# A top-10 index kernel: the last three tiles laid over 16 partitions a row, with a new order of the tail

## The chip, the cores and the metric

The kernel runs on one core of a Trainium2 chip. The metric is the device time of one execution in microseconds (us), and lower is better. The profiled span of a kernel is about 1.8 us shorter than its device time: the kernel before has 684.3 us in the profile and 686.1 us on the clock of that run. Times inside a profile count from the start of its span.

## The reference

For each of 8192 rows of 8192 random fp32 numbers: the indices of the ten largest, largest first.

```python
def reference(x, k):                       # x: (8192, 8192) fp32, k = 10
    indices = np.argpartition(x, -k, axis=1)[:, -k:]
    values = np.take_along_axis(x, indices, axis=1)
    sorted_idx = np.argsort(-values, axis=1)
    return np.take_along_axis(indices, sorted_idx, axis=1)   # int64
```

## The kernel before

The 64 tiles have 128 rows each (4.19 MB). A row lies over R = 8 partitions, W = 1024 numbers in each, so one SBUF tile holds S = 8 groups of A = 16 rows. A tile passes through these stages:

1. **Weigh.** ScalarE (ACT) takes exp(36 (x - 4.7)), and TensorE (PE) adds up those weights over the eight partitions of a row: 1024 chunk sums a row. A chunk with a large number in it has a large sum.
2. **Choose.** VectorE (DVE) takes the 12 best chunks of a row, in five passes over the sums.
3. **Gather, mask, extract.** GpSimd (POOL) fetches the eight numbers of each chosen chunk, DVE and POOL mask them to the row they belong to, and 12 small PE matmuls (24 rows of the profile; together the *extract* of a tile) bring them together: 12 x 8 = 96 candidates a row.
4. **Rank.** DVE takes the ten best candidates.
5. **Finish.** For a batch of eight tiles DVE turns positions into indices in seven steps; PE matmuls (the *deliveries*, two rows of the profile for each tile of the batch) bring them into rows of the output; a cast and a store follow.

The parts that the change and the argument touch, with cuts marked:

```python
epool = ...tile_pool(name="e", bufs=3)       # weights between ACT and PE: three buffers
xpool = ...tile_pool(name="x", bufs=4)       # x tiles
spsum = ... bufs=2    # chunk sums in PSUM
gpsum = ... bufs=3    # candidates in PSUM
fpsum = ... bufs=1    # the accumulator of the deliveries
starts = list(range(0, ntiles, TB)) + [last - 2]   # batches of 8; the last are 56-60 and 61-63

def load(t):
    src = x[t * P:(t + 1) * P, :].rearrange("(s a) (q j) -> (a q) s j", a=A, q=R)  # runs of 4 KB
    ...
def weigh(t):
    parts = [S // 4, S // 4, S // 4, S // 8, S // 8] if t == last else [S // 2, S // 2]
    for h, n in enumerate(parts):            # an ACT pass, then its matmuls
        e = epool.tile([P, S // 2, W], bf16, tag="e", name="e")
        nc.scalar.activation(out=e..., in_=xts[t]..., func=ACTF.Exp, ...)
        # n x 2 matmuls of 128x512 into the sums
...
    for t in range(last):                    # the order in which every engine gets its work
        interleave(choose_steps(t), rank_steps(t - LAG) if LAG <= t < last - 1 else [])
        if t >= 1:
            spread(t - 1, 0 if t == last - 1 else G // 2)      # the mask, DVE and POOL
        gather(t)
        weigh(t + 1)
        if 1 <= t < last - 2:
            extract(t - 1)
        todo = {last - 4: 5, last - 3: TB + 2}.get(t, 3)
        run(later[:todo])                    # finish steps and deliveries of a batch
        ...
    extract(last - 3)                        # tile 60
    extract(last - 2)                        # tile 61
    run(choose_steps(last)); spread(last - 1); gather(last)
    extract(last - 1)                        # tile 62
    # ranks of 59, 60, 61; seven finish steps of 56-60; mask, extract and rank of 63
    run(steps[-2:])                          # cast and store of 56-60
    run(finish_steps(batch_of[last]))        # 61-63
```

## Time and profile before

| | us |
|---|---|
| time, median of four runs | 686.68 (685.10 to 687.15) |
| profiled span | 684.3 |
| load of x at 420 GB/s, up to about | 645 |
| tail after it, about | 39 |
| in the tail: sums of tile 63 ready | 653.47 |
| indices of 63 given to POOL | 660.62 |
| extract of 63 done | 672.78 |
| last delivery done | 680.38 |

Up to about 645 us the load sets the pace: it runs at 420 GB/s while no engine is full (from 40 to 600 us PE and DVE are busy for 84% of the time, ACT for 75%). What a change of compute and its order can shorten is the tail. It is read as a chain of times at which the last tile (63) passes each stage.

### The profile page before, as it was taken

The page shows a single profiled execution, that of the slowest core. Times are in us where ns is not written, and L with a number is a line of the kernel's source. Part 1 is how long each engine was busy: PE and PEld are TensorE (multiplying, and loading weights), DVE is VectorE, ACT ScalarE, POOL GpSimd, SP SyncE. Part 2 cuts the span into 40 slices and gives each one's busy share as a digit, 9 for nine tenths or more (in the row PEclk, how much of TensorE's full clock was granted, in tenths as well). Part 3 has the DMA queues.
Part 4 walks back from the last instruction along what each step waited for, and adds up shares of the span by engine and source line. Part 5 has one row for each costly group of instructions (what it writes and reads, how often), then busy time and mean ns, then how long its engine had stood idle before and what let it go on. Part 6 is the DMA issues. An engine that isn't in the chain of part 4 may idle for free.

```text
span 684.3 us, 7927 instructions
## 1 busy us (share of the span) xinstructions
PE 555.2 (81%) x2646; PEld 342.9 (50%) x2690; DVE 559.3 (82%) x1313; ACT 488.8 (71%) x264; POOL 183.4 (27%) x135
## 2 busy tenths in 40 slices
PE   2688878888877788887988798889788788788976
PEld 0245544555554455554654456556445445445564
DVE  1567868799878977789896998789987898789996
ACT  5777777777777767777777777787777777777810
POOL 0113223313331331322331333132233133223250
PEclk9765866669888888596786667777988858866775
DMA  8999999999999999999999999999999999999700
GB/s 354 421 420 419 420 421 419 421 419 421 418 421 419 420 420 419 420 420 420 420 420 419 421 419 420 420 419 421 420 420 419 420 419 414 420 420 420 287 1 6
DMA packets 70592, 269.69 MB, mean 394 GB/s; under 512 B 4374, under 2 KB 5014, under 8 KB 70550
## 3 DMA queue, kind: packets, MB, share of 16 engines
q1 hardware_dynamic: 69926, 268.62, 95.9%
q10 hardware_dynamic: 624, 0.56, 0.3%
q8 instruction: 21, 0.34, 0.2%
q14 instruction: 21, 0.17, 0.1%
HBM read 268.51 MB, written 0.66 MB: 393 GB/s over the span
## 4 chain that ended last, share of the span: by engine, by line
DMA 58%; PE 14%; DVE 11%; SPq 5%; ACT 5%; issue 4%; POOL 2%; ACTq 0%; DVEq 0%
DMA xt<-in_x_dram 56%; PE s L152 8%; SPq L94 5%; ACT e L144 5%; PE g L214 4%; DVE wall L171 2%; DMA out_dram<-opack 2%; POOL cand L185 2%; DVE m L172 2%; DVE cidb L176 1%; DVE cidb L174 1%; PE fo L254 1%; DVE wall L175 1%; DVE masked L203 1%; DVE rows L274 0%
## 5 line engine op out<-in xcount | busy, mean ns | idle before, releaser
L144 ACT ACTIVATE e<-xt,bias 128x4096 bf16<-128x4096 f32 (+2 forms) x131 | 475.5, 3630 | 155.9 <-DMA xt<-in_x_dram 147.6
L152 PE MATMUL s<-e,group 128*128 128x512 bf16 x980 | 342.7, 506 | 117.4 <-ACT e L144 112.7
L152 PEld LDWEIGHTS <-group 128*128 128x128 bf16 x1024 | 123.8, 124 | 311.3 <-issue 259.5
L214 PEld LDWEIGHTS g<-cpack,masked 128*128 128x128 f32 x1536 | 207.7, 215 | 20.1 <-issue 9.0
L214 PE MATMUL g<-cpack,masked 128*128 128x8 f32 x1536 | 199.7, 269 | 4.9 <-DVE posb L228 3.1
L185 POOL INDIRECT_COPY cand<-xt,idx 128x192 f32 x64 | 64.8, 1013 | 478.9 <-DMA xt<-in_x_dram 123.6
L171 DVE MAX8 wall<-s 128x8 f32<-128x1024 f32 x64 | 78.8, 1232 | 114.0 <-PE s L152 102.7
L203 POOL TENSOR_TENSOR masked<-cand,cpack 128x768 f32<-128x768 f32 x64 | 117.6, 1838 | 5.3
L174 DVE FIND_INDEX8 cidb<-wall,s 128x8 uint16<-128x1024 f32 x64 | 78.4, 1224 | 0.0
L176 DVE FIND_INDEX8 cidb<-wall,m 128x8 uint16<-128x1024 f32 x64 | 78.1, 1220 | 0.0
L172 DVE MATCH_REPLACE8 m<-wall,s 128x1024 f32<-128x1024 f32 x64 | 77.8, 1215 | 0.0
L175 DVE MAX8 wall<-m 128x8 f32<-128x1024 f32 x64 | 77.4, 1209 | 0.0
L203 DVE TENSOR_TENSOR masked<-cand,cpack 128x768 f32<-128x768 f32 (+1 forms) x63 | 60.2, 956 | 0.2 <-POOL cand L185 0.2
L254 PE MATMUL fo<-rows,send 128*64 128x160 f32 (+2 forms) x128 | 28.4, 372 | 3.0 <-DVE rows L274 3.0
L144 ACT ACTIVATION_READ_ACCUMULATOR e<-xt,bias 128x1 f32 x131 | 24.4, 186 | 0.0
L254 PEld LDWEIGHTS fo<-rows,send 128*64 128x64 f32 (+2 forms) x128 | 18.4, 158 | 5.6 <-issue 3.5
L228 DVE FIND_INDEX8 posb<-t8a,g 128x8 uint16<-128x96 f32 x64 | 16.5, 258 | 0.0
L230 DVE FIND_INDEX8 posb<-t8b,g 128x8 uint16<-128x96 f32 x64 | 16.2, 254 | 0.0
L225 DVE MAX8 t8a<-g 128x8 f32<-128x96 f32 x64 | 15.9, 249 | 0.0
L226 DVE MATCH_REPLACE8 g<-t8a,g 128x96 f32<-128x96 f32 x64 | 15.9, 248 | 0.0
L336 ACT ACTIVATE e<-tall,bias 128x64 f32<-128x64 f32 x1 | 0.3, 347 | 21.5 <-DVE tall L231 21.5
L229 DVE MAX8 t8b<-g 128x8 f32<-128x96 f32 x64 | 15.6, 244 | 0.0
(37 smaller groups left out, 105.0 us busy)
## 6 DMA issues: line engine op xcount, KB each, us to landing
xt<-in_x_dram SPq DMA_DIRECT2D x248, 1024.0 KB, 16.3
xt<-in_x_dram SPq DMA_DIRECT2D x16, 512.0 KB, 9.2
out_dram<-opack ACTq DMA_DIRECT2D x6, 80.0 KB, 5.3
out_dram<-opack SPq DMA_DIRECT2D x1, 80.0 KB, 4.6
cpack<-topk_cpack ACTq DMA_DIRECT2D x1, 68.5 KB
out_dram<-opack SPq DMA_DIRECT2D x1, 50.0 KB
out_dram<-opack SPq DMA_DIRECT2D x1, 30.0 KB
```

Of the source, the lines that this page charges most:

```text
L94: nc.sync.dma_start(out=dst[:, s:s + n, :], in_=src[:, s:s + n, :])
L144: nc.scalar.activation(out=e[:, 0:n, :].rearrange("p s j -> p (s j)"), in_=xts[t][:, s0 * W:(s0 + n) * W], func=ACTF.Exp, bias=bias[:, 0:1 ...
L152: nc.tensor.matmul(ss[t][:, j:j + BANK], lhsT=group[:, s0 + i, :], rhs=e[:, i, j:j + BANK], start=s0 + i == 0, stop=s0 + i == S - 1)
L171: lambda: nc.vector.max(out=w16[:, 0:8], in_=m),
L172: lambda: nc.vector.match_replace(out=m2, in_to_replace=w16[:, 0:8], in_values=m, imm_value=-1.0),
L174: lambda: nc.vector.max_index(out=cid[:, 0:8], in_max=w16[:, 0:8], in_values=m),
L175: lambda: nc.vector.max(out=w16[:, 8:16], in_=m2),
L176: lambda: nc.vector.max_index(out=cid[:, 8:16], in_max=w16[:, 8:16], in_values=m2),
L185: nc.gpsimd.add_instruction(mybir.InstIndirectCopy(name=nc.get_next_instruction_name(), ins=[nc.gpsimd.lower_ap(xts[t]), nc.gpsimd.lower_a ...
L203: eng.tensor_tensor(out=masked[t][:, g0:g1], in0=cand[:, g0:g1].unsqueeze(2).to_broadcast(shape), in1=own.rearrange("p (c s) -> p c s", s= ...
L214: nc.tensor.matmul(gs[t][:, c, :], lhsT=mk[:, c, :, :].rearrange("p a s -> p (a s)"), rhs=place, start=True, stop=True)
L254: nc.tensor.matmul(fo, lhsT=send[:, i, 0:n * S], rhs=rows[:, i].rearrange("p a k -> p (a k)"), start=i == 0, stop=i == n - 1)
```

## The change

The intent, as far as the diff tells it: in the last three tiles, where nothing hides DVE's work, halve the number of chunk sums (a row over 16 partitions, 512 chunks of 16 numbers), so that choosing takes half as long. The price is 2 KB runs in the load and 192 candidates to rank. The last batch gets an accumulator of its own, in a buffer of the chunk sums, so that it need not wait for the cast of the batch before. The order of the tail changes too: extract 60 and the deliveries of batch 48-55 move ahead of the sums of tile 63. Smaller parts are the masks of the last tiles, shared out anew between DVE and POOL, and one buffer in place of two for the finish steps. The core of the diff, with cuts marked:

```diff
+class Layout:
+    def __init__(self, r):
+        self.R, self.A, self.S, self.W = r, P // r, r, N // r
...
+    wide, thin = Layout(8), Layout(16)
+    def layout(t):
+        return thin if t >= ntiles - TAIL else wide        # TAIL = 3
...
+        if b == len(starts) - 1:
+            fo = spsum.tile([P, wide.W], fp32, tag="s", name="fo")
+        else:
+            fo = fpsum.tile([P, wide.A * KMAX], fp32, tag="fo", name="fo")
...
-            interleave(choose_steps(t), rank_steps(t - LAG) if LAG <= t < last - 1 else [])
+            interleave(choose_steps(t), rank_steps(t - LAG) if t >= LAG else [])
             if t >= 1:
-                spread(t - 1, 0 if t == last - 1 else G // 2)
+                spread(t - 1)
             gather(t)
             weigh(t + 1)
-            if 1 <= t < last - 2:
+            if 1 <= t < last - 1:
                 extract(t - 1)
-            todo = {last - 4: 5, last - 3: TB + 2}.get(t, 3)
+            todo = {last - 4: 5, last - 3: 2}.get(t, 3)
+            if t == last - 2:
+                todo = TB
             run(later[:todo])
...
-        extract(last - 3)
-        extract(last - 2)
+        run(rank_steps(last - 3))
         run(choose_steps(last))
         spread(last - 1)
         gather(last)
+        extract(last - 2)
         extract(last - 1)
...
-        spread(last, 8)
+        run(steps[:5])
+        run(rank_steps(last - 2))
+        spread(last, G)
+        run(steps[5:7])
         extract(last)
...
+        final = finish_steps(batch_of[last])
+        run(final[:-2])
         run(steps[-2:])
+        run(final[-2:])
```

More of the change, by code (lines that the diff above doesn't have):

```diff
@@ L12 @@
 N = 8192
-R = 8
-A = P // R
-S = P // A
-W = N // R
 BANK = 512
@@ L26 @@
 LAG = 3
-PAD = 96
+TAIL = 3
+PAD = 208
+class Layout:
+    def __init__(self, r):
+        self.R, self.A, self.S, self.W = r, P // r, r, N // r
 @with_exitstack
@@ L57 @@
     out_u32 = out.bitcast(u32)
-    out_rows = out_u32.rearrange("(r a) n -> r (a n)", a=A)
+    wide, thin = Layout(8), Layout(16)
     consts = ctx.enter_context(tc.tile_pool(name="consts", bufs=1))
@@ L62 @@
     small = ctx.enter_context(tc.tile_pool(name="small", bufs=2))
-    bpool = ctx.enter_context(tc.tile_pool(name="batch", bufs=2))
+    bpool = ctx.enter_context(tc.tile_pool(name="batch", bufs=1))
     pad = ctx.enter_context(tc.tile_pool(name="pad", bufs=1)).tile([P, PAD], fp32, name="pad")
@@ L79 @@
     last = ntiles - 1
-    starts = list(range(0, ntiles, TB)) + [last - 2]
+    starts = list(range(0, ntiles, TB)) + [ntiles - TAIL]
     sizes = [b - a for a, b in zip(starts, starts[1:] + [ntiles])]
@@ L86 @@
     picked, ready = {}, {}
+    def layout(t):
+        return thin if t >= ntiles - TAIL else wide
     def load(t):
+        lay = layout(t)
         xts[t] = xpool.tile([P, N], fp32, tag="xt", name="xt")
-        src = x[t * P:(t + 1) * P, :].rearrange("(s a) (q j) -> (a q) s j", a=A, q=R)
-        dst = xts[t].rearrange("p (s j) -> p s j", j=W)
-        n = S // (8 if t in (0, last) else 4)
-        for s in range(0, S, n):
+        src = x[t * P:(t + 1) * P, :].rearrange("(s a) (q j) -> (a q) s j", a=lay.A, q=lay.R)
+        dst = xts[t].rearrange("p (s j) -> p s j", j=lay.W)
+        n = lay.S // (8 if t in (0, last) else 4)
+        for s in range(0, lay.S, n):
             nc.sync.dma_start(out=dst[:, s:s + n, :], in_=src[:, s:s + n, :])
@@ L99 @@
     part = np.arange(P)
-    own_np = (part[:, None] // R == part[None, :] // S).astype(np.float32)
-    place_np = (part[:, None] % R == np.arange(R)[None, :]).astype(np.float32)
-    base_np = ((part % S) * W).astype(np.float32)[:, None]
-    cpack_np = np.concatenate([own_np, place_np, base_np], axis=1)
-    cpack_dram = nc.inline_tensor(np.ascontiguousarray(cpack_np), name="topk_cpack")
-    cpack = consts.tile([P, P + R + 1], fp32)
+    packs, width = [], 0
+    for lay in (wide, thin):
+        lay.at = width
+        packs.append((part[:, None] // lay.R == part[None, :] // lay.S).astype(np.float32))
+        packs.append((part[:, None] % lay.R == np.arange(lay.R)[None, :]).astype(np.float32))
+        packs.append(((part % lay.S) * lay.W).astype(np.float32)[:, None])
+        width += P + lay.R + 1
+    cpack_dram = nc.inline_tensor(np.ascontiguousarray(np.concatenate(packs, 1)), name="topk_cpack")
+    cpack = consts.tile([P, width], fp32)
     nc.scalar.dma_start(out=cpack, in_=cpack_dram.ap())
-    own, place, base = cpack[:, 0:P], cpack[:, P:P + R], cpack[:, P + R:P + R + 1]
-    own_a = own.rearrange("p (a s) -> p a s", s=S)[:, :, 0]
     bias = consts.tile([P, 1], fp32)
@@ L113 @@
     nc.vector.memset(ones, 1.0)
-    group = consts.tile([P, S, P], bf16)
-    nc.vector.memset(group, 0.0)
-    for s in range(S):
-        nc.vector.tensor_copy(
-            out=group[:, s, :].rearrange("p (a s) -> p a s", s=S)[:, :, s], in_=own_a
-        )
-    send = consts.tile([P, TB, TB * S], fp32)
-    nc.vector.memset(send, 0.0)
-    for i in range(TB):
-        nc.vector.tensor_copy(out=send[:, i, i * S:(i + 1) * S], in_=place)
+    for lay, nsend in ((wide, TB), (thin, TAIL)):
+        R, A, S = lay.R, lay.A, lay.S
+        lay.own = cpack[:, lay.at:lay.at + P]
+        lay.own_a = lay.own.rearrange("p (a s) -> p a s", s=S)[:, :, 0]
+        lay.place = cpack[:, lay.at + P:lay.at + P + R]
+        lay.base = cpack[:, lay.at + P + R:lay.at + P + R + 1]
+        lay.group = consts.tile([P, S, P], bf16, name=f"group{R}")
+        nc.vector.memset(lay.group, 0.0)
+        for s in range(S):
+            nc.vector.tensor_copy(
+                out=lay.group[:, s, :].rearrange("p (a s) -> p a s", s=S)[:, :, s],
+                in_=lay.own_a,
+            )
+        lay.send = consts.tile([P, nsend, nsend * S], fp32, name=f"send{R}")
+        nc.vector.memset(lay.send, 0.0)
+        for i in range(nsend):
+            nc.vector.tensor_copy(out=lay.send[:, i, i * S:(i + 1) * S], in_=lay.place)
     slots_i = consts.tile([P, G], i32)
@@ L133 @@
     eall = consts.tile([P, nsums], fp32)
-    opacks = [consts.tile([TB * S, A, KMAX, 2], u32, name=f"opack{i}") for i in range(2)]
+    opacks = [consts.tile([TB * wide.S, wide.A, KMAX, 2], u32, name=f"opack{i}")
+              for i in range(2)]
     for o in opacks:
@@ L138, in weigh @@
     def weigh(t):
-        ss[t] = spsum.tile([P, W], fp32, tag="s", name="s")
+        lay = layout(t)
+        S, W = lay.S, lay.W
+        ss[t] = spsum.tile([P, wide.W], fp32, tag="s", name="s")[:, 0:W]
         parts = [S // 4, S // 4, S // 4, S // 8, S // 8] if t == last else [S // 2, S // 2]
@@ L142, in weigh @@
         for h, n in enumerate(parts):
-            e = epool.tile([P, S // 2, W], bf16, tag="e", name="e")
+            e = epool.tile([P, N // 2], bf16, tag="e", name="e")
             nc.scalar.activation(
-                out=e[:, 0:n, :].rearrange("p s j -> p (s j)"),
-                in_=xts[t][:, s0 * W:(s0 + n) * W],
+                out=e[:, 0:n * W], in_=xts[t][:, s0 * W:(s0 + n) * W],
                 func=ACTF.Exp, bias=bias[:, 0:1], scale=BETA,
@@ L151, in weigh @@
                 for j in range(0, W, BANK):
-                    nc.tensor.matmul(ss[t][:, j:j + BANK], lhsT=group[:, s0 + i, :],
-                                     rhs=e[:, i, j:j + BANK],
+                    nc.tensor.matmul(ss[t][:, j:j + BANK], lhsT=lay.group[:, s0 + i, :],
+                                     rhs=e[:, i * W + j:i * W + j + BANK],
                                      start=s0 + i == 0, stop=s0 + i == S - 1)
@@ L167, in choose_steps @@
         w16 = wall[:, t, :]
-        m2 = small.tile([P, W], fp32, tag="m2", name="m2")
+        lay = layout(t)
+        m2 = small.tile([P, wide.W], fp32, tag="m2", name="m2")[:, 0:lay.W]
         idxs[t] = small.tile([P, G], u16, tag="idx", name="idx")
@@ L177, in choose_steps @@
             lambda: nc.vector.tensor_scalar(
-                out=idxs[t], in0=cid[:, 0:G], scalar1=float(W - 1), scalar2=base,
+                out=idxs[t], in0=cid[:, 0:G], scalar1=float(lay.W - 1), scalar2=lay.base,
                 op0=ALU.min, op1=ALU.add,
@@ L205, in spread @@
                 in0=cand[:, g0:g1].unsqueeze(2).to_broadcast(shape),
-                in1=own.rearrange("p (c s) -> p c s", s=16).unsqueeze(1).to_broadcast(shape),
+                in1=layout(t).own.rearrange("p (c s) -> p c s", s=16).unsqueeze(1).to_broadcast(shape),
                 op=ALU.mult,
@@ L211, in extract @@
         mk = masked.pop(t)
-        gs[t] = gpsum.tile([P, G, R], fp32, tag="g", name="g")
+        gs[t] = gpsum.tile([P, G * thin.R], fp32, tag="g", name="g")
+        R = layout(t).R
         for c in range(G):
-            nc.tensor.matmul(gs[t][:, c, :], lhsT=mk[:, c, :, :].rearrange("p a s -> p (a s)"),
-                             rhs=place, start=True, stop=True)
+            nc.tensor.matmul(gs[t][:, c * R:(c + 1) * R], lhsT=mk[:, c, :, :].rearrange("p a s -> p (a s)"),
+                             rhs=layout(t).place, start=True, stop=True)
     def rank_steps(t):
-        g = gs.pop(t).rearrange("p c q -> p (c q)")
+        n = G * layout(t).R
+        g = gs.pop(t)[:, 0:n]
         b = batch_of[t]
@@ L222, in rank_steps @@
         t8b = small.tile([P, 8], fp32, tag="t8b", name="t8b")
-        g2 = small.tile([P, G * R], fp32, tag="g2", name="g2")
+        g2 = small.tile([P, G * thin.R], fp32, tag="g2", name="g2")[:, 0:n]
         return [
@@ L238, in finish_steps @@
         n = sizes[b]
+        lay = layout(starts[b])
+        R, A, S, W = lay.R, lay.A, lay.S, lay.W
         r0 = starts[b] * S
+        out_rows = out_u32.rearrange("(r a) n -> r (a n)", a=A)
         queue = nc.sync if b >= len(starts) - 3 else nc.scalar
@@ L246, in finish_steps @@
         val = bpool.tile([P, TB, KMAX], fp32, tag="val", name="val")[:, 0:n, :]
-        rows = bpool.tile([P, TB, A, KMAX], fp32, tag="rows", name="rows")[:, 0:n]
-        fo = fpsum.tile([P, A * KMAX], fp32, tag="fo", name="fo")[0:n * S, :]
-        o = opacks[b % 2][0:n * S]
+        rows = bpool.tile([P, TB, wide.A, KMAX], fp32, tag="rows", name="rows")[:, 0:n, 0:A]
+        if b == len(starts) - 1:
+            fo = spsum.tile([P, wide.W], fp32, tag="s", name="fo")
+        else:
+            fo = fpsum.tile([P, wide.A * KMAX], fp32, tag="fo", name="fo")
+        fo = fo[0:n * S, 0:A * KMAX]
+        o = opacks[b % 2][0:n * S, 0:A]
         hshape = [P, n, KMAX, G]
@@ L253, in move @@
         def move(i):
-            nc.tensor.matmul(fo, lhsT=send[:, i, 0:n * S],
+            nc.tensor.matmul(fo, lhsT=lay.send[:, i, 0:n * S],
                              rhs=rows[:, i].rearrange("p a k -> p (a k)"),
@@ L275, in finish_steps @@
                 out=rows, in0=val.unsqueeze(2).to_broadcast(rshape),
-                in1=own_a.unsqueeze(1).unsqueeze(3).to_broadcast(rshape), op=ALU.mult),
+                in1=lay.own_a.unsqueeze(1).unsqueeze(3).to_broadcast(rshape), op=ALU.mult),
         ] + [lambda i=i: move(i) for i in range(n)] + [
@@ L318 @@
         gather(last)
+        extract(last - 2)
         extract(last - 1)
-        run(rank_steps(last - 4))
-        run(rank_steps(last - 3))
-        run(rank_steps(last - 2))
+        run(later)
         nc.vector.tensor_scalar(
@@ L326 @@
         steps = finish_steps(batch_of[last - 3])
-        spread(last, 8)
+        run(steps[:5])
+        run(rank_steps(last - 2))
+        spread(last, G)
+        run(steps[5:7])
         extract(last)
-        run(steps[:7])
+        run(steps[7:-2])
         run(rank_steps(last - 1))
-        run(steps[7:-2])
         run(rank_steps(last))
+        nc.scalar.activation(out=e10, in_=tall, func=ACTF.Exp, bias=bias[:, 0:1], scale=BETA)
+        final = finish_steps(batch_of[last])
+        run(final[:-2])
         run(steps[-2:])
-        nc.scalar.activation(out=e10, in_=tall, func=ACTF.Exp, bias=bias[:, 0:1], scale=BETA)
-        run(finish_steps(batch_of[last]))
+        run(final[-2:])
         nc.vector.scalar_tensor_tensor(
@@ L344 @@
     nc.vector.reduce_sum(out=ngood1, in_=good, axis=X_AX)
-    gps = fpsum.tile([P, A * KMAX], fp32, tag="fo", name="gps")[0:1, 0:1]
+    gps = fpsum.tile([P, wide.A * KMAX], fp32, tag="fo", name="gps")[0:1, 0:1]
     nc.tensor.matmul(gps, lhsT=ngood1, rhs=ones, start=True, stop=True)
```

## The prediction

> **What bounds the kernel now.** I read the page first. Its slices show a DMA that is full until the last three slices, while no engine is:
>
> ```profile
> DVE  1567868799878977789896998789987898789996
> ACT  5777777777777767777777777787777777777810
> PEclk9765866669888888596786667777988858866775
> DMA  8999999999999999999999999999999999999700
> GB/s 354 421 420 419 420 421 419 421 419 421 418 421 419 420 420 419 420 420 420 420 420 419 421 419 420 420 419 421 420 420 419 420 419 414 420 420 420 287 1 6
> ```
>
> The 268 MB of x come at 420 GB/s, one tile of 128 rows (4.19 MB) in 9.98 us, and no compute change can shorten that stretch. Then I read busy times of each engine by stretch, to find where the load ends:
>
> ```profile
> 630.00:640.00 10.00, 8.81 (x41) 5.04 (x39) 9.97 (x22) 7.54 (x4) 2.81 (x2) 0.66 1.03 417
> 640.00:646.00 6.00, 5.85 (x26) 3.93 (x27) 6.00 (x17) 5.19 (x3) 2.83 (x2) 0.72 0.78 302
> 646.00:652.00 6.00, 4.70 (x22) 1.86 (x20) 4.64 (x8) 6.00 (x9) 2.52 (x2) 1.00 0.11 34
> 658.00:673.00 15.00, 11.94 (x57) 11.78 (x57) 14.22 (x51) 0.00 (x0) 5.81 (x4) 0.50 0.00 1
> 673.00:684.00 11.00, 4.55 (x18) 2.44 (x16) 4.86 (x21) 0.35 (x1) 0.00 (x0) 0.50 0.03 8
> ```
>
> The columns are PE, PE weight loads, DVE, ACT, POOL, then granted clock, DMA share and GB/s. The load is over near 645 us; the span is 684.3 us. So about 39 us of tail follow, and the change aims at that tail alone. Last I read the tail in order of time:
>
> ```profile
> 639.96 3.70 PE L254 MATMUL fo<-rows,send 128*64 128x160 f32 x16
> 643.60 4.80 PE L152 MATMUL s<-e,group 128*128 128x512 bf16 x19
> ...
> 653.98 1.23 DVE L171 MAX8 wall<-s 128x8 f32<-128x1024 f32 x1
> ...
> 660.30 0.32 DVE L177 TENSOR_SCALAR idx<-cidb,cpack 128x12 uint16<-128x12 uint16 x1
> ...
> 662.40 10.38 PE L214 MATMUL g<-cpack,masked 128*128 128x8 f32 x48 [3.06 <-DVE posb L228]
> ...
> 664.85 1.01 POOL L185 INDIRECT_COPY cand<-xt,idx 128x192 f32 x1 [4.25 <-DVE g L226]
> 665.89 1.23 DVE L203 TENSOR_TENSOR masked<-cand,cpack 128x1024 f32<-128x1024 f32 x1 [0.23 <-POOL cand L185]
> ...
> 675.64 0.32 DVE L278 CAST opack<-fo 40x160 uint32<-40x160 f32 x1 [1.38 <-PE fo L254]
> ...
> 680.41 0.31 DVE L278 CAST opack<-fo 24x160 uint32<-24x160 f32 x1 [1.95 <-PE fo L254]
> ```
>
> The reader is to see one chain: choose the last tile on DVE (653.98 to 660.62), gather it on POOL (to 665.86; the record of 1.01 us is only its end), mask it, extract on PE until 672.78, rank on DVE to 674.27, wait for the delivery matmuls of the batch before (to 675.64), finish the last batch on DVE (675.88 to 678.47), deliver (to 680.38), cast, store, 684.3. Call the last three tiles 61, 62 and 63.
>
> [...]MAX8: 1232 ns at 1024 elements and 249 at 96, so 1.06 ns an element and about 147 ns fixed. [...]read in stretches of 1 us, the clock is full from 637.4 to 640.9 and from 644.3 to 657.9, then half to the end. Extracts keep PE busy[...]: 24 took 3.0 us at full and about 4.9 at half. [...]from its indices to its end the gather of tile 62 took 4.65 us with no two-input DVE work beside it, that of tile 63 5.24 beside 0.94 us of it, that of tile 59 6.7 beside 2.8 us. [...]x has 4 KB runs now and none of 2 KB in bulk[...].
>
> **The change, part by part.**
>
> 1. Halved chunk sums. Five DVE passes of a tile go from 1024 to 512 elements[...]. Choosing tile 63 falls from 6.64 to 3.97 us. For 61 and 62 it is DVE time beside other work, and worth something only if DVE is what tile 63 waits for. Before, it was so by a hair: PE had the sums of 63 at 653.5, DVE came free at 653.9.
>
> 2. The price of 16 partitions. x for three tiles comes in 2 KB runs[...]. Ranking sees 192 and not 96 candidates: 5 x 0.1 = 0.5 us a tile, 1.35 becomes 1.85. The constants grow by 74 KB, 0.2 us of DMA. Chunk-sum matmuls and extracts stay as many; extracts have 16 columns, not 8, and I leave them at their price[...]. The base of the x buffers stays a multiple of 512 bytes, so I expect no change in the steady rate.
>
> 3. The new PE order. Before, PE did the 16 delivery matmuls of the batch 48-55 ahead of tile 62's sums, and the extracts of 60 and 61 after tile 63's sums. Now PE's program reads: sums of 62, extract 60, 16 delivery matmuls, sums of 63, extracts 61, 62, 63. So work of 3.0 + 2.4 = 5.4 us (full clock: 0.15 each delivery; at half 0.28) lies between the sums of 62 and of 63. The second half of 62 leaves ACT at about 645.0[...]. PE: its sums to 646.9, extract to 649.9, deliveries to 652.3, first quarter of 63 to 653.2. ACT has only three e buffers, so its fourth part of 63 waits for that quarter: 653.3 to 654.5, the fifth to 655.7, last sums 656.3. Before: 653.5. This gives back nearly all of part 1: choosing 63 runs 656.4 to 660.4, against 660.62.
> If the clock drops to half for the deliveries it is about 1.7 us later, and if PE never warms before 653 about 4.8 us later.
>
> 4. Gather of 63. In its 4.65 us now fall the mask of 62 (0.95) and two passes of the batch's one-hot (about 0.8 and 0.5, between the 80-row and 30-row prices): 2.2 us of two-input work, by the ratio above about 1.6 us more, so 6.2 against 5.24. It ends at 666.6.
>
> 5. Mask and extract of 63. All 12 slots on DVE[...], to 668.4. Extract 62 no longer stands in front: rank 59 now comes early, so its buffer is free (the 3.06 us wait goes), and it runs in the gather. Extract 63 at half clock 4.9, to 673.3. Before: 672.78.
>
> 6. The end. Rank 63: 1.85, to 675.1. The last batch needs no wait for the cast of the batch before, having its own accumulator: 1.6 us saved. Seven DVE steps: 2.59 less 0.25 (rows shrink from 480 to 240 elements) = 2.35, to 677.5. Delivery with 80 columns and not 160: 1.3 with the wait, to 678.8, against 1.9 before. The rest as before, 684.3 - 680.38 = 3.92: 682.7.
>
> Sum of this best-clock course against before: choosing -0.2, gather +1.0, mask and extract -0.3, rank +0.4, wait -1.6, DVE steps -0.25, delivery -0.6: about -1.6 us.
>
> **The rivals.** (a) PE's clock stays low between 644 and 653 and the sums of 63 come late: +0.1 us in all if it drops for the deliveries, +3.2 if it never warms.[...] (b) The author's saving stands: if ACT and PE are nimbler than I think and the sums of 63 come at 654, the halved passes count in full, -2.3 us more: -3.9. The order was surely chosen for some gain, so I give this weight. (c) 2 KB runs cost 10%[...]: 3 us later arrival, of which ACT, waiting on x until 640.8, would pass on about 2: +0.5 to +1. No run shows it. (d) Nothing in the body moves, so a gain over 2% (13.7 us of a 39 us tail) would need over a third of the tail, which no sum here comes near; a loss of that size would need the load to slow, which the kept alignment speaks against.
>
> **Range and chances.** Best-clock course -1.6, middle +0.1, cold +3.2, author's gain -3.9, weighed 0.35, 0.25, 0.15 and 0.25: -1.0 us. 686.68 - 1.0 = 685.7. The range holds (b) at its full size and the cold course but for its last 0.7 us, with some room on the low side: 682.4 to 689.2. Faster by over 2% 0.01, within 2% 0.98, slower 0.01.
>
> **What would show it right or wrong.** Right: choosing MAX8 over 512 elements at 0.69 us; the sums of 63 ending at 656 to 658; ACT's fourth part of 63 idle for PE some 2.5 us; the gather of 63 over 6 us; no DVE wait for the delivery between rank 63 and the last seven steps; GB/s at 420 up to 630 us. Wrong: the sums of 63 ready by 654, a load of the last three tiles that ends over 2 us later, an extract of 63 at full clock (3.0 us, end 2 us sooner), or a body whose rate differs from 420 GB/s, which would outweigh the whole tail.

The course above comes to -1.6 us and the weighed forecast to 685.7 us with terms in them whose working no trace of the kernel before shows: the rate behind the halved passes (part 1), the later arrival of x in 2 KB runs (part 2; it is also in the 645.0 of part 3) and the formula of the mask (part 5). For the first and the last the trace gives nearly the same: at its 1.06 ns an element five halved passes save 2.7 us, so choosing takes 3.9, and from the masks of 768 and 1024 elements (0.956 and 1.23 us) one of 1536 is estimated at 1.78 us. What 2 KB runs cost was not shown; it stood in the forecast as the author's estimate. What sets the clock was not shown. That the place of the x buffers matters is shown by calls 1 and 2 below, for 64 bytes: 409 GB/s against 420.

## The result, and the profile after

The kernel after takes 687.19 us (median of four runs, 686.26 to 687.66), the kernel before 686.68 in the same rounds. The ratio is 1.001, with a 95% interval of 0.999 to 1.003: the same. A ratio here is the mean time of one kernel's fast runs over the mean of the other's of the same rounds, so it is not quite the ratio of the medians. The output is right. The profiled execution of the kernel after was the slowest of its four, with a span of 685.8 us against 684.3, so the tail below shows 1.5 us more, where the medians differ by 0.5.

From the page of the kernel after, the granted clock and the DMA rate in 40 slices of the span:

```profile
PEclk9976698867878688676877889677789768778675
GB/s 352 420 421 420 420 421 419 420 419 420 420 420 420 419 420 420 421 419 421 420 420 419 420 419 420 420 420 421 420 421 419 422 416 418 419 417 386 293 5 6
```

The body runs at 420 GB/s as before, with x buffers that begin at a multiple of 512 bytes as before; 64 bytes more gave 409 (call 1). Slices 37 and 38 differ: 386 and 293 here, 420 and 287 before. Those hold the load of the last three tiles in 2 KB runs. By stretches (start:end and length in us, then busy time and count of PE, PE weight loads, DVE, ACT and POOL, granted clock, DMA share, GB/s), first the kernel before:

```profile
610.00:620.00 10.00, 8.80 (x40) 4.88 (x40) 7.92 (x20) 7.64 (x5) 2.62 (x3) 0.66 1.02 421
620.00:630.00 10.00, 8.60 (x40) 4.86 (x40) 9.93 (x23) 7.63 (x5) 1.49 (x1) 0.66 1.02 421
```

then the kernel after:

```profile
610.00:620.00 10.00, 10.00 (x52) 6.57 (x52) 7.83 (x20) 7.60 (x4) 3.71 (x4) 0.74 1.02 401
620.00:630.00 10.00, 5.80 (x39) 4.03 (x37) 9.93 (x21) 7.56 (x4) 1.32 (x2) 0.95 1.03 381
630.00:640.00 10.00, 8.45 (x28) 3.95 (x27) 9.09 (x22) 7.47 (x5) 2.64 (x2) 0.54 1.05 408
...
652.00:656.00 4.00, 4.00 (x18) 2.78 (x17) 3.01 (x13) 0.00 (x0) 0.00 (x0) 0.60 0.00 0
656.00:663.00 7.00, 6.08 (x39) 4.16 (x37) 4.01 (x15) 2.37 (x4) 2.56 (x2) 0.98 0.05 12
663.00:680.00 17.00, 13.37 (x58) 12.13 (x58) 13.24 (x44) 0.35 (x1) 1.01 (x1) 0.50 0.00 1
```

The DMA is as busy as before and moves less: over these 30 us 1190 against 1259 when the three rates are added, 5.5% less, or 0.69 MB, which is 1.65 us at 420 GB/s. The loss is uneven: 377 GB/s from 618 to 630 us and 406 from 630 to 644 (in a3_standin, below, 380 and 406). PE is busy for all of 652 to 656 at a mostly halved clock (0.60) while ACT does nothing, although the load is over (57 GB/s from 646 to 652, nothing from 652). From 656 to 663 the clock is nearly full (0.98), from there to 680 it is half, so extract 63 runs at half clock, as it did before. The tail in order of time (start, duration, engine, line, operation, tiles and sizes; in brackets the idle time of the engine before it and what ended it) shows why. First two rows of the kernel before, where ACT did not wait ahead of its fourth part of tile 63:

```profile
650.48 1.13 ACT L144 ACTIVATE e<-xt,bias 128x1024 bf16<-128x1024 f32 x1
...
652.88 0.59 PE L152 MATMUL s<-e,group 128*128 128x512 bf16 x2 [0.54 <-ACT e L144]
```

then selected rows of the kernel after:

```profile
645.41 3.57 PE L169 MATMUL s<-e,group 128*128 128x512 bf16 x8 [1.53 <-ACT e L162]
648.78 3.05 PE L233 MATMUL g<-cpack,masked 128*128 128x8 f32 x24
651.76 3.53 PE L281 MATMUL fo<-rows,send 128*64 128x160 f32 x16
655.22 3.68 PE L169 MATMUL s<-e,group 128*128 128x512 bf16 x14
656.83 1.15 ACT L162 ACTIVATE e<-xt,bias 128x1024 bf16<-128x1024 f32 x1 [5.51 <-issue]
659.25 0.59 PE L169 MATMUL s<-e,group 128*128 128x512 bf16 x2 [0.35 <-ACT e L162]
659.88 0.70 DVE L189 MAX8 wall<-s 128x8 f32<-128x512 f32 x1 [2.89 <-PE s L169]
663.48 0.23 DVE L195 TENSOR_SCALAR idx<-cidb,cpack 128x12 uint16<-128x12 uint16 x1
668.66 1.01 POOL L203 INDIRECT_COPY cand<-xt,idx 128x192 f32 x1 [8.28 <-DVE t8b L249]
671.61 5.28 PE L233 MATMUL g<-cpack,masked 128*128 128x16 f32 x24 [1.62 <-DVE val L299]
678.84 0.17 DVE L286 TENSOR_SCALAR slot<-posb 128x30 uint16<-128x30 uint16 x1
681.31 0.62 PE L281 MATMUL fo<-rows,send 128*48 128x80 f32 x6 [1.61 <-DVE rows L301]
```

The reader is to see the first five rows of the kernel after as one jam. PE's program puts extract 60 (648.78) and the deliveries of batch 48-55 (651.76, 16 rows) between the last sums of tile 62 and the first of tile 63. ACT has filled its three weight buffers and stands still for 5.51 us, until PE has used the first quarter of tile 63. The releaser column says "issue", which here is only that no event was recorded on that wait. So the sums of 63 are ready at 659.84 (659.25 + 0.59), 6.4 us later than before. The halved choosing then takes 3.83 us (659.88 to 663.71) and not 6.64, and the row at 678.84 has no bracket: DVE goes from the rank straight to the last batch, where it had waited for the cast of the batch before.

The tail as a ledger, with each stage's end in us. "Step" is what a stage adds to or takes from the difference between the kernels. The prediction's columns are those of its best-clock course.

| stage of tile 63 | before | after | step measured | predicted | step predicted |
|---|---|---|---|---|---|
| chunk sums | 653.47 | 659.84 | +6.4 | 656.3 | +2.8 |
| choosing | 660.62 | 663.71 | -3.3 | 660.4 | -3.0 |
| gather | 665.86 | 669.67 | +0.7 | 666.6 | +1.0 |
| mask and extract | 672.78 | 676.89 | +0.3 | 673.3 | -0.2 |
| rank | 674.27 | 678.86 | +0.5 | 675.1 | +0.3 |
| last batch starts | 675.88 | 678.84 | -1.6 | 675.1 | -1.6 |
| seven DVE steps | 678.47 | 681.26 | -0.2 | 677.5 | -0.2 |
| delivery | 680.38 | 681.93 | -1.2 | 678.8 | -0.6 |
| end of span | 684.3 | 685.8 | 0.0 | 682.7 | 0.0 |
| sum | | | +1.5 | | -1.6 |

The two sums differ by 3.1 us. The chunk sums alone came 3.6 us later than the best course had them; the other rows together give back 0.5.

### The profile page after: what moved, and what is told of

The parts are those of the page before. It is cut to its first block, busy times and chain, and to the rows that moved or that the text cites. A ratio compares the mean times of both kernels' runs of the same rounds, so it can differ in the third digit from the quotient of the medians.

```text
span 685.8 us, 7990 instructions
## 1 busy us (share of the span) xinstructions
PE 553.5 (81%) x2690; PEld 340.7 (50%) x2690; DVE 556.0 (81%) x1335; ACT 488.8 (71%) x264; POOL 179.0 (26%) x134
## 4 chain that ended last, share of the span: by engine, by line
DMA 55%; DVE 13%; PE 13%; ACT 6%; SPq 5%; issue 5%; POOL 2%; ACTq 0%; DVEq 0%
DMA xt<-in_x_dram 53%; PE s L169 9%; ACT e L162 6%; SPq L101 5%; PE g L233 3%; DVE wall L189 3%; POOL cand L203 2%; DMA out_dram<-opack 2%; DVE m L190 2%; DVE cidb L194 1%; DVE cidb L192 1%; DVE masked L221 1%; DVE wall L193 1%; DVE pick L298 1%; DVE t8a L245 0%
## 5 line engine op out<-in xcount | busy, mean ns | idle before, releaser
L233 PE MATMUL g<-cpack,masked 128*128 128x8 f32 (+1 forms) x1536 | 199.3, 269 | 4.5 <-DVE masked L221 2.9
L189 DVE MAX8 wall<-s 128x8 f32<-128x1024 f32 (+1 forms) x64 | 77.2, 1207 | 119.1 <-PE s L169 119.1
L192 DVE FIND_INDEX8 cidb<-wall,s 128x8 uint16<-128x1024 f32 (+1 forms) x64 | 76.6, 1197 | 0.0
L194 DVE FIND_INDEX8 cidb<-wall,m 128x8 uint16<-128x1024 f32 (+1 forms) x64 | 76.4, 1193 | 0.0
L190 DVE MATCH_REPLACE8 m<-wall,s 128x1024 f32<-128x1024 f32 (+1 forms) x64 | 76.1, 1189 | 0.0
L193 DVE MAX8 wall<-m 128x8 f32<-128x1024 f32 (+1 forms) x64 | 75.6, 1182 | 0.0
L221 DVE TENSOR_TENSOR masked<-cand,cpack 128x768 f32<-128x768 f32 x64 | 61.5, 960 | 0.9 <-POOL cand L203 0.9
L245 DVE MAX8 t8a<-g 128x8 f32<-128x96 f32 (+1 forms) x64 | 16.1, 252 | 2.5 <-PE g L233 2.5
L248 DVE FIND_INDEX8 posb<-t8a,g 128x8 uint16<-128x96 f32 (+1 forms) x64 | 16.6, 260 | 0.0
L250 DVE FIND_INDEX8 posb<-t8b,g 128x8 uint16<-128x96 f32 (+1 forms) x64 | 16.4, 256 | 0.0
```

What stands on the lines that cost most here:

```text
L189: lambda: nc.vector.max(out=w16[:, 0:8], in_=m),
L190: lambda: nc.vector.match_replace(out=m2, in_to_replace=w16[:, 0:8], in_values=m, imm_value=-1.0),
L192: lambda: nc.vector.max_index(out=cid[:, 0:8], in_max=w16[:, 0:8], in_values=m),
L193: lambda: nc.vector.max(out=w16[:, 8:16], in_=m2),
L194: lambda: nc.vector.max_index(out=cid[:, 8:16], in_max=w16[:, 8:16], in_values=m2),
L221: eng.tensor_tensor(out=masked[t][:, g0:g1], in0=cand[:, g0:g1].unsqueeze(2).to_broadcast(shape), in1=layout(t).own.rearrange("p (c s) -> ...
```

## The experiments

**The theory.** The author's gain is real, and PE's new order gives it back: extract 60 and the deliveries ahead of the sums of 63 make those sums late, through PE's program order and ACT's three weight buffers. Then the new order alone, on the old layout, must cost about 3 us, and the deliveries put back on the new kernel must gain about as much. **The rivals.** (1) The late sums cost nothing, because DVE or POOL would not be ready for them. (2) The work that was moved costs the same wherever it stands, since PE is then the bound after the sums. (3) The 2 KB runs eat the gain.

**The stand-in.** The experiments could not use GpSimd's indirect copy, so every kernel below has other POOL work in place of the gather, made to take about as long. Their results are wrong (99% of the indices). With wrong data the kernel's own check would start its slow path, so its last test compares with 1000 and the slow path is never taken. It took three stand-ins until the pair behaved like the real one, and the first two taught something too. The kernels named s, b (before) and a (after) carry a stand-in alone. Each call ran on one chip, with the real kernel before in the same rounds.

| call | run | edit | median us | ratio to the kernel before, 95% |
|---|---|---|---|---|
| 1 | s_before | stand-in 1 | 706.80 | 1.0289 (1.0273 to 1.0305) |
| 1 | s_after | stand-in 1 | 704.65 | 1.0249 (1.0231 to 1.0268) |
| 1 | e1_old_order | s_after, old order of extract 60 and deliveries | 704.59 | 1.0249 (1.0232 to 1.0265) |
| 1 | e2_new_order | s_before, new order of both | 708.36 | 1.0320 (1.0302 to 1.0338) |
| 2 | b2_standin | stand-in 1, pad 64 bytes shorter | 690.29 | 1.0046 (1.0031 to 1.0061) |
| 2 | a2_standin | the same on the kernel after | 684.65 | 0.9956 (0.9940 to 0.9972) |
| 2 | a2_deliv | a2_standin, deliveries back | 682.71 | 0.9930 (0.9915 to 0.9944) |
| 2 | b2_new_order | b2_standin, new order | 690.37 | 1.0050 (1.0033 to 1.0067) |
| 3 | b3_standin | stand-in 3 | 687.22 | 1.0002 (0.9979 to 1.0024) |
| 3 | a3_standin | stand-in 3 | 687.16 | 1.0002 (0.9980 to 1.0025) |
| 3 | a3_deliv | a3_standin, deliveries back | 683.41 | 0.9953 (0.9927 to 0.9979) |
| 3 | b3_new_order | b3_standin, new order | 690.64 | 1.0044 (1.0024 to 1.0064) |

The kernel before had medians of 687.01, 687.06 and 687.27 in the three calls.

### Call 1: a stand-in with a fill

```diff
-        idxs[t] = small.tile([P, G], u16, tag="idx", name="idx")
+        idxs[t] = small.tile([P, G], fp32, tag="idx", name="idx")
...
-        nc.gpsimd.add_instruction(mybir.InstIndirectCopy(...))
+        nc.gpsimd.tensor_tensor(out=xts[t][:, 0:G], in0=xts[t][:, G:2 * G], in1=idxs[t], op=ALU.mult)
+        nc.gpsimd.memset(xts[t][:, N - FILL:N], 0.0005)              # FILL = 3456
+        nc.gpsimd.tensor_tensor(out=cands[t], in0=xts[t][:, N - 16 * G:N]..., in1=idxs[t]..., op=ALU.mult)
...
-    with tc.If(passed < checks):
+    with tc.If(passed < 1000):
```

> Stand-in for the kernel before: the gather, which may not be run again, is replaced by a small multiply that reads the indices, a fill of 3456 elements and a multiply of 192 elements on the same engine, so that some 4.5 us pass between indices and candidates; results are wrong on purpose and the slow path is never taken. Expected: within 0.5% of 686.7 us, the load at 420 GB/s, the sums of tile 63 complete near 653.5 us, the choosing of 63 starting when DVE comes free near 654. If the stand-in is far longer or shorter than the gather (under 3.5 or over 5.5 us), the pair must be calibrated again.

Measured: 706.80 us, 20 us over the real kernel, which is far too much for a stand-in that takes about as long as the gather. The page says where it went:

```profile
GB/s 346 410 410 408 408 410 408 409 409 409 408 410 409 409 410 407 410 409 409 408 411 408 409 408 410 409 409 410 409 409 410 409 409 407 409 409 409 218 0 6
```

The whole load runs at 409 GB/s and not 420. The index tiles had become fp32, so the x buffers behind them in SBUF now began 64 bytes beyond a multiple of 512, where those of the real kernel begin at one. The pair can still be compared with itself, and call 2 tests the alignment.

> The same stand-in in the changed kernel. Expected: the ratio to the stand-in of before within 0.4% of 1.00 (the two originals: 1.001), the sums of tile 63 near 659 to 660 us, and ACT's fourth part of tile 63 idle about 5 us for PE, as in the changed kernel. If the ratio is off by over 0.6%, the stand-in does not carry the argument.

Measured: 704.65, some 2.2 us under s_before where the real pair is level. ACT's idle time ahead of its fourth part of tile 63 was 2.38 us and not about 5: the slower load had brought ACT later, and extract 60 and the deliveries ran at full clock (2.74 and 2.39 us).

In e1_old_order the extracts and the deliveries of the kernel after stand where they stood before:

```diff
-            if 1 <= t < last - 1:
+            if 1 <= t < last - 2:
                 extract(t - 1)
-            todo = {last - 4: 5, last - 3: 2}.get(t, 3)
-            if t == last - 2:
-                todo = TB
+            todo = {last - 4: 5, last - 3: TB + 2}.get(t, 3)
...
-        run(rank_steps(last - 3))
+        extract(last - 3)
         run(choose_steps(last))
         spread(last - 1)
         gather(last)
+        run(rank_steps(last - 3))
```

> Changed kernel with stand-in, but PE's old order: deliveries of the batch 48-55 ahead of the sums of tile 62, extract 60 after the sums of tile 63, and rank 60 moved behind the choosing of 63 so that DVE does not wait for it. My theory (the gain is given back by PE's order): ACT's idle time before the fourth part of 63 disappears, sums of 63 complete near 654.5 us, choosing of 63 starts near 655, and the span falls 3.5 to 5 us below the changed stand-in (0.5 to 0.7%). Rival (the slower arrival of 2 KB runs holds the sums of 63 back): sums of 63 near 657 or later and a fall under 2 us. Rival (PE is then the bound, with extracts 60, 61 and 62 in front of extract 63): choosing early, but extract 63 ends no earlier than 675.

Measured: 704.59, no gain over s_after, although in the profiles the sums of 63 came at 672.9 and not at 675.5. PE in time, e1_old_order:

```profile
672.76 13.57 PE L232 MATMUL g<-cpack,masked 128*128 128x8 f32 x72
688.19 5.27 PE L232 MATMUL g<-cpack,masked 128*128 128x16 f32 x24 [1.87 <-DVE val L298]
```

and s_after:

```profile
686.24 5.28 PE L232 MATMUL g<-cpack,masked 128*128 128x16 f32 x24 [0.62 <-DVE val L298]
```

Extract 63 starts 1.95 us later than in s_after, and two things hold it back. The one that came last is DVE, which works without a wait from 672.96 until the mask of 63 is done: the rank of 60 has moved behind the choosing (1.4 us), and in this stand-in POOL holds up DVE's mask of tile 62 (2.31 us where s_after has 0.95) and its 16-bit passes (some 1.5 us). That part is the stand-in's doing. The other is PE itself: three extracts in a row, at a mostly halved clock (0.50 from 680 us), keep it until 686.33 (672.76 + 13.57), 0.1 us past the time at which s_after began extract 63. So even a DVE that was ready would have found no gain here, and rival (2) holds for the whole old order in this run: extract 60 behind the sums shifts PE's jam to the other side of them. The gain of 3.5 to 5 us that was expected did not come. The deliveries remained to be tested alone.

e2_new_order is the opposite edit on s_before: extract 60 and the deliveries go ahead of the sums of 63 (the same lines reversed, `extract(last - 3)` taken from its place after the loop).

> Kernel before with stand-in, wide layout and one accumulator for all, but PE's new order: deliveries of the batch 48-55 and extract 60 between the sums of 62 and of 63. My theory: ACT idles 4 to 5.5 us for PE, sums of 63 complete near 658 to 659 us, and the span grows 4 to 6 us (0.6 to 0.9%) over the stand-in of before. Rival (the delay comes from 2 KB runs or from the 16 chunk weights of the new layout): no growth over 1 us.

Measured: 708.36, 1.6 us over s_before, with ACT idle for 4.49 us. The direction is the theory's, the size is not; but both kernels loaded at 409 GB/s.

### Call 2: the same stand-in on aligned x buffers

```diff
-PAD = 96
+PAD = 80
```

These are 16 floats, 64 bytes less in front of the x buffers; the kernel after goes from 208 to 192 likewise.

> Stand-in of the kernel before, with the padding shortened by 64 bytes so that the four x buffers begin at multiples of 512 bytes again (the first stand-ins had them 64 bytes past, and loaded at 409 GB/s). If the alignment is the cause of the slow load: 420 GB/s in the body and a time within 1% of the kernel before (686 to 692 us). Rival (the fills of the stand-in slow the load): still 409 GB/s and some 706 us.

Measured: 690.29 us, 16.5 us less than s_before, with the load at 420 GB/s again and not 409. Nothing else differs between these two kernels, so the 64 bytes are shown to be the cause. Other places were not run.

> Stand-in of the changed kernel, aligned likewise. Expected: within 0.4% of the aligned stand-in of before (originals 1.001), GB/s 420 until the last three tiles and about 390 there, ACT idle 4 to 6 us before its fourth part of tile 63.

Measured: 684.65, which is 5.6 us under b2_standin. So the pair with stand-in 2, which was expected to be level, is not, and does not reproduce the real pair. The groups of b2_standin point to why. The columns are count, then busy us and mean ns of one, then idle before it:

```profile
L261 DVE TENSOR_SCALAR low<-posb 128x80 uint16<-128x80 uint16 x7 | 21.4, 3058 | 0.0
```

This 16-bit pass of DVE took 172 ns in the kernel before. Here it stands for 3058 ns, beside POOL's fill of 2979 ns. DVE was therefore late with tile 62 and began to choose tile 63 at 656.42, a microsecond after the sums (655.33). A stand-in must match not only the duration but also what it holds up.

> Aligned stand-in of the changed kernel with one part of the order undone: the 16 delivery matmuls of the batch 48-55 stand ahead of the sums of tile 62 again; extract 60 stays between the sums of 62 and 63. My theory: only 3 to 5 us of PE work are left between, so ACT's idle time falls from about 5 to 1 to 2 us, the sums of 63 come about 3 us earlier and the span falls 2.5 to 3.5 us (0.4 to 0.5%). Rival (2 KB arrival or DVE holds 63 back): ACT idle falls but the span moves under 1 us.

The edit is the deliveries alone, on a2_standin:

```diff
-            todo = {last - 4: 5, last - 3: 2}.get(t, 3)
-            if t == last - 2:
-                todo = TB
+            todo = {last - 4: 5, last - 3: TB + 2}.get(t, 3)
             run(later[:todo])
```

Measured: 682.71, 1.9 us under a2_standin (2.5 to 3.5 expected), with the sums of 63 at 654.6 and not 657.7. In the profile of a2_standin the clock was full for extract 60 and for the deliveries (2.74 and 2.39 us), and ACT was idle for 3.54 us; but it was half (0.50 from 641 to 646) for most of the sums of 62.

> Aligned stand-in of the kernel before with only the new PE order. My theory: sums of 63 come 3 to 5 us later; of that 2 to 4 us reach the end, since the wide choosing and the deferred ranks leave some slack. The misaligned pair showed sums 2.6 us later and 1.6 us in the time, where the slower load left PE more room. Rival (the order is harmless): under 1 us.

Measured: 690.37, level with b2_standin, although the sums of 63 came 3.1 us later. This looks like rival (1). That the fill had already made DVE late in b2_standin takes up 1.0 us of it: in the traces choosing 63 still starts 2.1 us later (658.48 against 656.42) and the span is 1.3 us longer, which the medians don't show. So this run speaks against the theory with stand-in 2, and the rest of it stays unexplained; call 3 repeats it with a stand-in that leaves DVE on time.

### Call 3: a stand-in that holds nobody up

```diff
+        for c in range(CHAIN):                       # CHAIN = 14, each waits for the one before
+            nc.gpsimd.tensor_tensor(out=xts[t][:, (c + 1) * G:(c + 2) * G],
+                                    in0=xts[t][:, c * G:(c + 1) * G], in1=idxs[t], op=ALU.add)
+        nc.gpsimd.tensor_tensor(out=cands[t], in0=tiny..., in1=idxs[t]..., op=ALU.mult)
```

`tiny` is a constant; PAD is 64 and 176, so that the x buffers stay aligned.

> Third stand-in of the kernel before. The fill of the second one held DVE's 16-bit passes back (a pass of 0.17 us took 3.06), so the gather is now 14 small dependent adds and a multiply on the same engine[...]; x buffers aligned to 512 bytes. Expected: 4.3 to 5.5 us from indices to candidates, 16-bit DVE passes back under 0.4 us, time within 0.5% of the kernel before, the last sums of tile 63 near 653.5 us.

Measured: 687.22, ratio 1.0002. From its indices to its end the stand-in of tile 63 takes 5.16 us (the real gather 5.24), the 16-bit pass takes 171 ns, and the sums of 63 are ready at 653.56 (653.47). (The two pairs of numbers are the stand-in's and the real kernel's.)

> The same stand-in in the changed kernel. Expected: within 0.4% of its partner (originals 1.001), ACT idle 4 to 6 us for PE before the fourth part of 63, sums of 63 near 658 to 660 us.

Measured: 687.16, ratio 1.0002. The pair is level, like the real one, and the stand-in of 63 takes 5.84 us (the real gather 5.97). ACT and DVE in time, a3_standin:

```profile
656.54 1.15 ACT L165 ACTIVATE e<-xt,bias 128x1024 bf16<-128x1024 f32 x1 [5.20 <-issue]
659.59 0.70 DVE L192 MAX8 wall<-s 128x8 f32<-128x512 f32 x1 [2.56 <-PE s L172]
```

In PE's rows, extract 60 and the deliveries stand between the sums of 62 and of 63:

```profile
645.43 3.52 PE L172 MATMUL s<-e,group 128*128 128x512 bf16 x8 [1.52 <-ACT e L165]
...
648.79 2.74 PE L235 MATMUL g<-cpack,masked 128*128 128x8 f32 x24
...
651.46 3.86 PE L283 MATMUL fo<-rows,send 128*64 128x160 f32 x16
```

The stall of ACT (5.20 us; 5.51 in the real kernel) and the start of choosing (659.59; 659.88) are those of the kernel after. On this pair the theory can be tested.

a3_deliv is the edit of a2_deliv, on a3_standin.

> The changed kernel with the third stand-in and the 16 delivery matmuls put back ahead of the sums of 62. My theory, and what the second stand-in gave (sums of 63 3.1 us earlier, median 1.9 us lower): ACT's idle time falls to under 2 us, sums of 63 come 2.5 to 4 us earlier, the time falls 1.5 to 3.5 us. Rival (the gain is lost elsewhere): sums earlier but the time moves under 0.7 us.

Measured: 683.41, 3.75 us under a3_standin (medians) and ratio 0.9953 to the kernel before (the interval leaves out 1). One of its six runs was 687.55 at a mean clock of 0.763, the other five 682.89 to 684.14 at 0.772 to 0.782; all are in the ratio. The same places in time, a3_deliv:

```profile
640.51 2.39 PE L283 MATMUL fo<-rows,send 128*64 128x160 f32 x16
...
645.28 1.89 PE L172 MATMUL s<-e,group 128*128 128x512 bf16 x8 [0.55 <-ACT e L165]
...
647.00 2.74 PE L235 MATMUL g<-cpack,masked 128*128 128x8 f32 x24
...
649.60 5.30 PE L172 MATMUL s<-e,group 128*128 128x512 bf16 x15
...
652.62 1.15 ACT L165 ACTIVATE e<-xt,bias 128x1024 bf16<-128x1024 f32 x1 [0.30 <-ACT e L165]
...
654.94 0.70 DVE L192 MAX8 wall<-s 128x8 f32<-128x512 f32 x1 [1.03 <-PE s L172]
```

The deliveries run at 640.51, ahead of the sums of tile 62, and PE's wait for the weights of the second half of 62 shrinks from 1.52 to 0.55 us. After extract 60 PE goes straight to the sums of 63, ACT's stall has shrunk from 5.20 to 0.30 us, and choosing starts 4.65 us earlier, of which 4.2 us reach the end of the span (681.2 against 685.4).

Not all of the 4.65 us is the place of the deliveries. Their own time is 3.8 us (651.46 to 655.26), of which about 1.0 is given back, since the sums of 63 now wait for ACT. The other 1.6 us is the clock: the second half of 62's sums took 1.72 us up to the next row (clock 1.00) and not 3.36 (0.50). The clock of a3_deliv stood at 1.00 from 637 us on, before the moved deliveries, where a3_standin had 0.50 until 638; a2_deliv shows 1.00 up to 649 too. Whether the new place of the deliveries holds the clock up, or these profiled runs happened to have it, was not separated.

b3_new_order is the opposite: extract 60 and the deliveries ahead of the sums of 63, on the old layout.

```diff
-            if 1 <= t < last - 2:
+            if 1 <= t < last - 1:
                 extract(t - 1)
-            todo = {last - 4: 5, last - 3: TB + 2}.get(t, 3)
+            todo = {last - 4: 5, last - 3: 2}.get(t, 3)
+            if t == last - 2:
+                todo = TB
...
-        extract(last - 3)
         extract(last - 2)
```

> The kernel before with the third stand-in and the new PE order alone. With the second stand-in the sums of 63 came 3.1 us later and the time did not move, and there DVE was 2.5 us late anyway because of the fill. My theory: without that distortion the sums come 3 to 4.5 us later and 1 to 4 us reach the end. Rival (wide layout hides the order): sums later, the time moves under 0.7 us.

Measured: 690.64, 3.4 us over b3_standin (medians), ratio 1.0044. ACT, DVE and PE in time, b3_new_order:

```profile
655.91 1.15 ACT L147 ACTIVATE e<-xt,bias 128x1024 bf16<-128x1024 f32 x1 [5.24 <-issue]
...
658.97 1.23 DVE L174 MAX8 wall<-s 128x8 f32<-128x1024 f32 x1 [4.16 <-PE s L155]
...
667.31 10.38 PE L216 MATMUL g<-cpack,masked 128*128 128x8 f32 x48 [5.80 <-DVE posb L230]
```

and b3_standin, where DVE waited for nothing there:

```profile
654.34 1.22 DVE L174 MAX8 wall<-s 128x8 f32<-128x1024 f32 x1
```

The same stall of ACT appears (5.24 us) with 1024 sums and 4 KB runs, and DVE stands idle for 4.16 us. Extracts 62 and 63 start at 667.31, where b3_standin started them at 662.68. So the order alone costs 3.4 us, and rivals (1) and (3) are out as the main cause: late sums do cost, and without any 2 KB run. The clock differs between the two runs as well: from 646 to 652 us it was 0.78 in b3_new_order and 1.00 in b3_standin, and the second half of 62's sums took 3.08 us up to the next row, where a3_deliv took 1.72 at 1.00. Whether the order brought this about was not separated.

**What the three calls settle.** The order, with the clock seen beside it, costs about 3.4 us on the old layout; as the pair is level, the rest of the change gains about as much. The part of the order that can be taken back with profit is the deliveries; taking extract 60 back as well gained nothing in e1_old_order, though on the first stand-in only. The version with the deliveries back was 0.5% faster than both kernels with stand-in 3. With the real gather it has not been run, so its gain there is an expectation, not a result. The 2 KB load alone and the second accumulator alone were not run either; what is said of them is read from the two traces.

## Why the prediction was right, and where it was off

The prediction was 685.7 us, "the same" at 0.98, and the result is 687.19 us, within the range (682.4 to 689.2). Its mechanism, that PE's new order gives back nearly all of the halved choosing, is shown by a3_deliv and b3_new_order, on stand-ins. "The same" alone proves little: all four courses that the prediction weighed, from -3.9 to +3.2 us, lie within 2%. By its own steps:

1. **Halved sums: right.** Choosing took 3.83 us where it gave 3.97. MAX8 over 512 sums took 700 ns where it gave 0.69 us.
2. **The price: one term too small.** What the prediction put down for 2 KB runs was not shown by a trace; it was less than the 1.65 us over 30 us that was measured. Most of it was hidden: the second half of tile 62 began on ACT at 641.56 against 640.81, 0.75 us later, and in tile 63 ACT stood for PE and not for x. Rival (c), 10% and 3 us, was right for the rate from 618 to 630 us (377 against 421 GB/s), too high for the whole (5.5%), and wrong in what it does to the end. The rank took 1.94 us where it gave 1.85.
3. **PE's order: right mechanism, wrong size. This is the step that missed.** The best-clock course had "last sums 656.3" and the fourth part of ACT idle for about 2.5 us; measured were 659.84 and 5.51. PE's rows give the parts of these 3.5 us: the first matmul of tile 62's second half came at 645.41 and not at 645.0 (+0.4); its sums took 3.37 us up to the next row and not 1.9 (+1.5), at half clock; the deliveries took 3.46 and not 2.4 (+1.1), at half clock from 653 us; the first quarter of 63 up to ACT's release took 1.6 and not 1.0 (+0.6); extract 60 took the 3.0 it was given. So most of the 3.5 us is clock: 2.6 us in two groups that ran at 0.50 wholly (643 to 649) or in their later part (653 to 656), and most of the 0.6 behind them. Where the clock was 1.00 the same rows took 1.72 us (the sums, a3_deliv) and 2.39 us (16 deliveries, a2_standin); at 0.50 ten deliveries took 2.89 us (672.71 in the kernel before). The prediction's other two courses, 658.0 and 661.1 for the sums, enclose the measured value, with ends of +0.1 and +3.2 us; the measured +1.5 in the profiled pair lies between them. Rival (a) is the one that came true, and 0.35 was too much for the best course. In a2_standin, where the clock was full for extract and deliveries but half for most of the sums of 62, those ended at 648.55 and not at 646.9, and the sums of 63 came at 657.7. No run here had the new order with a full clock all through, so the best course itself was not tested.
4. **Gather: right within 0.3 us.** The gather of 63 took 5.96 us, 6.2 predicted ("over 6" among its signs), with 2.25 us of two-input DVE work inside it (the mask of tile 62 and two one-hot passes), 2.2 predicted. In the kernel before it took 4.65 us for tile 62 with none of it inside and 5.24 for tile 63 with 0.94 us. No run isolates this.
5. **Mask and extract: right in the parts.** The mask took 1.76 us, as predicted. The extract ran at half clock, as predicted, but took 5.28 us; the prediction's "about 4.9 at half" misreads its own trace. The row to read it from is the kernel before's pair of extracts at half clock, 10.38 us for two, 5.19 each, so the 16 columns in place of 8 cost only 0.1. In that row PE is busy for 10.38 us without a break at a clock of 0.50 all through; at 1.00 one extract took 2.74 us (648.55 in a2_standin). The 3.06 us wait for the buffer of tile 62's extract is gone.
6. **The end: right.** No wait between the rank and the last batch (-1.6 as predicted), seven steps in 2.4 us (2.35 predicted). The delivery gained 1.2 us and not 0.6. Here luck helped: the clock was 1.00 from 681 us, and its rows took 0.62 us; in a3_deliv, at 0.50, they took 1.03.

Rival (b), that the author's saving stands in full with sums at 654, is false for the kernel as it was changed, and close to true for a3_deliv, where the sums come at 654.9. Rival (d) is right: no slice of the body up to 610 us moved by more than 4 GB/s. "GB/s at 420 up to 630 us" was wrong: it was 401 and 381 from 610 to 630, where the 2 KB runs already come in.

## What to carry to other kernels

A shorter step on the critical path is worth only what its input's arrival leaves of it: here choosing became 2.8 us shorter and its sums came 6.4 us later. Look at what stands ahead of the last input in the program of the engine that makes it (here 6.4 us of PE work, from 648.78 to 655.22), and put work that nobody waits for ahead of a point at which its engine waits anyway (here the deliveries, ahead of a wait of 1.52 us that shrank to 0.55). Moving a whole group of work can hide this: here one part (the deliveries) belonged elsewhere and the other (the extract) did not, which only separate runs tell. A stand-in for an instruction is a measuring tool and has to be checked as one: against the span of the original, against the load rate (409 and not 420 GB/s in call 1), and against what runs beside it (a DVE pass of 3058 ns and not 172 in call 2).
